# Grouping small matrix products by the shape of the array's parts in a three-block network

## The chip, the cores and the metric

The kernel runs on one core of one Trainium2 chip. The metric is the device time of one execution in microseconds (us). TensorE (PE) multiplies matrices: a weight load (PEld) puts the left operand into the array, a matmul streams the right operand through it. VectorE (DVE), ScalarE (ACT) and GpSimd (POOL) work beside it, and SyncE (SP) issues the transfers. Every engine takes its instructions in the order of the program.

## The reference

The network has three parts over 512 tokens of 1024 features, all in float32: a block with neighbourhood attention, a short convolution and an MLP; a layer of RWKV-7 time mixing between two gated MLPs; and a layer of sliding-window attention with sinks between two gated MLPs. The change concerns the RWKV scan above all. Its recurrence, per head of 64 features (16 heads):

```
def step(S, inp):
    r_t, w_t, k_t, v_t, kk_t, b_t = inp
    sa = jnp.einsum('bhij,bhj->bhi', S, -kk_t)
    S = (S * w_t[:, :, None, :] + sa[..., None] * b_t[:, :, None, :]
         + v_t[..., None] * k_t[:, :, None, :])
    y = jnp.einsum('bhij,bhj->bhi', S, r_t)
    return S, y
```

Around it stand the projections of r, k, v, low-rank decays and gates, a group norm per head, and an output projection.

## The kernel before

Activations lie with features on the 128 partitions and tokens along the free axis. The large products split each float32 operand into a high and a low part of a faster type (`wh`, `wl` for weights; three products for one); in the trace these are the rows `m<-a,wh`, `m<-a,wl`, `m<-wh,a`. Here they are called the main products.

The scan is done in chunks of 64 tokens (`c` = 0 to 7) for each half of the heads (`q` = 0, 1), so in 16 steps. A half of the heads is four pairs `p`, and a pair is two heads `e` = 0 and 1, which lie on partitions 0 to 63 and 64 to 127. There are three parts, each a task of its own:

- Block preparation, `prep(q, j)` for each block `j` of 128 tokens (lines 1354 to 1430). VectorE makes the scaled operands `bk` and `ee` (the tile `E[q, e, cg]`) for a chunk; TensorE multiplies them, four products per head (line 1404, operands on 64 partitions, 128 columns); VectorE masks the result into `ARB` and `E`. There are 16 such chunks, with eight products each.
- `inverse(j)` (lines 1445 to 1505): GpSimd inverts small triangular blocks in 62 operations, transfers bring the result through DRAM (`fsc`, `iat`, `xsc`), and TensorE joins the blocks with products of 32 x 32. The scan of block `j` waits for it.
- `scan_task(q)` (lines 1568 to 1649). A step makes a right-hand side (line 1595, eight products), multiplies with the inverse (line 1603, eight), makes the next state (line 1620, eight), and the output `y` of the chunk (lines 1636 to 1641): for each head and pair one product with 128 rows and 64 columns of the array (`ee` with `sv`) and, added to it, one with 64 rows and 64 columns (`ARB` with `uv`). So `y` has eight products of each of the two shapes. The two heads' outputs lie in two banks of PSUM, on the same 64 partitions. Such a float32 product has two records in the trace.

In the RWKV part all this runs among the main products of the projections, and later among those of the following MLP. The order on TensorE is set before the run by a planner, the class `_Emit`: it follows a coarse clock for TensorE and lanes for the others, and resumes a task when its clock reaches the time at which the tiles that the task named are expected. `mm` (line 363) and `transpose` (line 375) advance TensorE's clock by a duration that they state; so a changed duration can move every instruction of the program. A framework below it, which schedules by priority, may still move single instructions.

Of the kernel before, what the change touches and what calls it, by code (L numbers as in the profile page):

```python
# [13 lines left out]
F32R = mybir.dt.float32r  # L14
# [4 lines left out]
PSUM = bass.MemoryType.PSUM  # L19

P = 128
T = 512
D = 1024
# [37 lines left out]
class _Lane:  # L61
    """the busy spans of an engine; an operation takes the time that is free from when it is ready"""
# [25 lines left out]
class _Emit:  # L88
    """Order of emission for TensorE, which runs its instructions in the order in which they are emitted.

    A coarse model follows when each tile's contents will be there. The main thread of matrix products
    advances the clock of TensorE; side tasks are generators that yield a delay, or the tiles that their
    next instructions need, and are resumed when the clock gets there."""
# [4 lines left out]
    def __init__(self):  # L98
# [6 lines left out]
        self.urgent = 0  # L105

# [14 lines left out]
    def avail(self, aps):  # L121
        """when TensorE can read, or for a bank of PSUM write, these"""
        return max((self.slot.get(ap.tensor.name, 0.0) if ap.space == PSUM else self.ready([ap]) for ap in aps), default=0.0)

    def new(self, ap, tag):
        """a tile's slot is free once the tile that had it is done with"""
# [24 lines left out]
    def gate(self, outs, t):  # L151
        """tiles of a tag get their slots in the order of emission"""
        return max([t] + [self.seq.get(ap.tensor.tag, 0.0) for ap in outs if self.is_new(ap)])
# [49 lines left out]

    def pe(self, out, ins, dur):
# [33 lines left out]
    def need(self, *aps):  # L238
        """side tasks take the time until these tiles are ready"""
# [16 lines left out]
class _Engine:  # L256
    """an engine whose instructions the emission's model follows"""
# [25 lines left out]
def tile_net(ctx: ExitStack, tc: tile.TileContext, a: dict, out: bass.AP, dbg=None, stop=None):  # L283
# [26 lines left out]
    def free(*tiles, n=0):  # L310
        """these tiles of apool have had their last use, and n unnamed ones"""
# [15 lines left out]
    def PS(side=None):  # L327
        """a bank of PSUM; those of the side tasks are apart, for banks are handed out in the order of emission"""
# [33 lines left out]

    def mm(out_, lhsT, rhs, start=True, stop=True):
# [5 lines left out]
        em.pe(out_, [lhsT, rhs], 0.0025 + (max(n, 2 * m if m > 64 else m) if rhs.dtype == F32R else max(n, m) * (3 if m == 64 else 4)) / 2400.0)  # L369
# [6 lines left out]
    def transpose(out_, in_):  # L376
        nc.tensor.transpose(out_, in_, ident[: in_.shape[0], : in_.shape[0]])  # L377
        em.pe(out_, [in_], 0.11)

# [37 lines left out]
    def gemm(ps, w, n, ks, xs, cols=FULL, first=None, last=None, eng=None):  # L417
        """ps[:, cols] += W[ks, row block n]^T @ xs[cols] for a weight laid out [n, 128, k * 128]"""
# [7 lines left out]
    def gemm_head(w, ns, xs, ready):  # L426
        """the first row blocks of a product, a half of the tokens at a time as xs becomes ready"""
# [12 lines left out]
    def gemm_n(pss, w, xs, js=range(4), ncol=512, first={}):  # L440
        """token-major: pss[j] = xs[:, block j]^T @ W for W laid out [128, k * ncol]; first: those of W loaded before"""
# [14 lines left out]
    def rsqrt_(y, v, tmp):  # L456
        """y = v ** -0.5 (v > 0) on small tiles"""
# [7 lines left out]
    class Stat:  # L465
        """sum of squares over features, and from it each token's (mean + eps) ** -0.5"""
# [52 lines left out]
    def when(cond, fn):  # L519
        """run fn once cond holds"""  # L520
# [6 lines left out]
    def attention(units, depth):  # L527
        """softmax attention, a few units of a head and a block of queries in flight; a unit is a generator"""
# [13 lines left out]
    # =====================================================================  # L542
    # first block (tokens column-major: t' = col * 8 + row)
    # =====================================================================
# [1582 lines left out]
```

## Time and profile before

| | us |
|---|---|
| median of 3 runs | 3050.56 (3047.28 to 3051.03) |
| span of the profiled execution, first to last instruction | 3042.9 |
| TensorE busy | 2896.4 (95%) |
| VectorE busy | 1630.0 (54%) |
| ScalarE busy | 1255.6 (41%) |
| GpSimd busy | 694.0 (23%) |

The profiled execution has its own time as a span alone; it lies 7.7 us below the median of the runs. Matmuls overlap in the array, so the start of the next row tells more of a product's cost than its own duration. From about 1060 to 1800 us the RWKV layer runs; before and after it lie attention and MLPs.

### The profile page before, as it was taken

Reading aid. Unit: us, or ns where it says so; the run is one execution under the profiler, and the core shown is the slowest. Engines: PE = TensorE matmul, PEld = TensorE weight load, DVE = VectorE, ACT = ScalarE, POOL = GpSimd, SP = SyncE. Lnnn points to the kernel's source line nnn. Section 1 sums busy time; section 2 is a strip of 40 time slices with the busy share of each in tenths; the row PEclk is TensorE's granted clock in tenths of the full one; section 3 lists DMA queues with packets and bytes.
Section 4 is the critical chain, followed back from the end, with each engine's and each line's share of the span. In section 5 each row is a group of like instructions: output and inputs, shape, how many; then the busy total and the mean of one; then the engine's idle time right before and its main releaser. Section 6 shows DMA issues by size and latency. Waiting matters only on the chain. (4 is left out here: it accounts for less than half of the span.)

```text
span 3042.9 us, 45860 instructions
## 1 busy us (share of the span) xinstructions
PE 2896.4 (95%) x17744; PEld 2490.5 (82%) x17744; DVE 1630.0 (54%) x2920; ACT 1255.6 (41%) x2205; POOL 694.0 (23%) x809
## 2 busy tenths in 40 slices
PE   9999999999999988888889999998999989899998
PEld 7788988889788876667678999998888886788887
DVE  6554443335334596855774575457334475752336
ACT  4532333333433345544454444344323347643333
POOL 0011211112211153562173110011111135320111
PEclk9999999999999989897888999999999999999999
DMA  5333333332233456554564455442333433323334
GB/s 177 86 97 97 111 97 97 97 97 91 90 98 125 127 180 198 180 154 141 161 190 118 158 171 178 124 158 84 111 99 123 122 101 84 97 82 100 107 111 156
DMA packets 179409, 378.32 MB, mean 124 GB/s; under 512 B 57204, under 2 KB 81908, under 8 KB 179192
## 3 DMA queue, kind: packets, MB, share of 16 engines
q1 hardware_dynamic: 179192, 375.40, 40.0%
q8 instruction: 140, 2.29, 0.3%
q14 instruction: 77, 0.63, 0.1%
HBM read 342.04 MB, written 29.36 MB: 122 GB/s over the span
## 5 line engine op out<-in xcount | busy, mean ns | idle before, releaser
L364 PE MATMUL m<-a,wh 128*128 128x256 f32 (+1 forms) x8512 | 2075.8, 335 | 13.6 <-DVE a L275 5.9
L364 PEld LDWEIGHTS m<-a,wh 128*128 128x128 f32 x8512 | 1469.0, 193 | 179.3 <-issue 10.9
L364 PE MATMUL m<-a,wl 128*128 128x256 f32 (+1 forms) x4256 | 1418.6, 334 | 1.0 <-DVE wl L275 1.0
L275 ACT ACTIVATE wh<-wr 128x1024 fp32r<-128x1024 f32 (+2 forms) x585 | 606.4, 1038 | 1228.6 <-PE m L364 855.6
L275 DVE TENSOR_TENSOR wl<-wr,wh 128x1024 fp32r<-128x1024 f32 (+2 forms) x547 | 674.9, 1236 | 480.2 <-ACT wh L275 477.2
L364 PEld LDWEIGHTS m<-a,wl 128*128 128x128 f32 x4256 | 819.6, 193 | 78.1 <-issue 2.4
L275 POOL TENSOR_TENSOR a<-a,a 128x256 f32<-128x256 f32 (+5 forms) x319 | 363.6, 1147 | 1552.6 <-ACT a L275 1328.6
L275 DVE TENSOR_TENSOR a<-m,a 128x512 f32<-128x512 f32 (+1 forms) x324 | 208.7, 645 | 642.2 <-PE m L364 624.5
L275 ACT ACTIVATE a<-a 128x512 f32<-128x512 f32 (+6 forms) x531 | 253.1, 494 | 127.5 <-DVE a L275 108.2
L364 PE MATMUL m<-wh,a 128*128 128x512 f32 x800 | 269.3, 410 | 16.7 <-ACT a L275 8.7
L364 PEld LDWEIGHTS m<-wh,a 128*128 128x128 f32 x800 | 155.7, 195 | 56.6 <-ACT a L275 10.2
L275 DVE TENSOR_TENSOR a<-a,a 128x256 f32<-128x256 f32 (+3 forms) x305 | 174.6, 598 | 28.9 <-ACT a L275 22.2
L364 PE MATMUL m<-wl,a 128*128 128x512 f32 x400 | 161.6, 404 | 3.7 <-DVE wl L275 2.3
L275 DVE SCALAR_TENSOR_TENSOR a<-a,vec,a 128x256 f32<-128x256 f32 (+4 forms) x246 | 144.7, 628 | 8.6 <-ACT a L275 8.3
L275 POOL TENSOR_TENSOR a<-h,a 128x256 fp32r<-128x256 f32 x80 | 68.6, 861 | 302.6 <-ACT a L275 294.4
L275 POOL TENSOR_TENSOR wl<-wr,wh 128x1024 fp32r<-128x1024 f32 x38 | 93.8, 2471 | 143.5 <-ACT wh L275 136.7
L364 PE MATMUL t<-a,a 64*128 64x128 f32 (+3 forms) x400 | 85.1, 358 | 14.6 <-DVE a L275 12.9
L364 PEld LDWEIGHTS m<-wl,a 128*128 128x128 f32 x400 | 78.5, 196 | 20.8 <-DVE wl L275 3.4
L364 PE MATMUL t<-sv,a 128*64 128x64 f32 x992 | 89.5, 245 | 0.0
L364 PEld LDWEIGHTS t<-sv,a 128*64 128x64 f32 x992 | 67.4, 142 | 23.4 <-issue 3.8
L275 ACT ACTIVATE a<-t 128x512 f32<-128x512 f32 (+3 forms) x122 | 58.9, 491 | 65.5 <-PE t L364 53.5
L364 PEld LDWEIGHTS t<-a,a 64*128 64x128 f32 (+2 forms) x400 | 54.4, 204 | 33.3 <-issue 19.8
(109 smaller groups left out, 1595.5 us busy)
## 6 DMA issues: line engine op xcount, KB each, us to landing
wr<-in_ffn_w_in_dram SPq DMA_DIRECT2D x204, 512.0 KB, 3.6
wr<-in_ffn_w_out_dram SPq DMA_DIRECT2D x80, 448.0 KB, 3.3
wr<-in_ffn_w_out_dram SPq DMA_DIRECT2D x48, 512.0 KB, 3.5
wr<-in_w_out_t_dram SPq DMA_DIRECT2D x34, 512.0 KB, 3.3
wr<-in_w_mlp_in_dram SPq DMA_DIRECT2D x32, 512.0 KB, 3.6
wr<-in_w_mlp_out_dram SPq DMA_DIRECT2D x32, 512.0 KB, 3.7
wr<-in_w_gate_dram SPq DMA_DIRECT2D x16, 512.0 KB, 3.5
wr<-in_w_k_dram SPq DMA_DIRECT2D x16, 512.0 KB, 5.1
```

The costliest lines, as they stand in the source:

```text
L275: return fn(*args, **kw)
L364: nc.tensor.matmul(out_, lhsT=lhsT, rhs=rhs, start=start, stop=stop)
```

## The change

In the scan, the 16 products of a step's output are written in another order: first the eight with 128 rows, then the eight with 64 rows, the two heads alternating in each. The accumulation's start stands at the first pair alone and its stop at the last. In the block preparation, the eight products of a chunk are issued after one wait for both heads' operands, the heads alternating, into two banks. And the planner's price of a product changes: a new function adds 0.09 us where the shape of the array's part differs from that of the product before, and halves the duration where the shape is the same and the place another; the discount for 64 columns goes. Comments were removed as well, which shifts the line numbers (the products' line 364 is 377 now, the transposes' 377 is 391).

```diff
+        self.shape, self.pos = (128, 128), (0, 0)
...
+    def tile_time(self, out, lhsT, dur):
+
+        rows, cols = (ap.ap[0][1] for ap in (lhsT, out))
+        shape = (64 if rows == 64 else 32 if rows <= 32 else 128, 64 if cols == 64 else 32 if cols <= 32 else 128)
+        pos = (lhsT.offset // lhsT.ap[0][0], out.offset // out.ap[0][0])
+        if shape != self.shape:
+            dur += 0.09
+        elif pos != self.pos:
+            dur *= 0.5
+        self.shape, self.pos = shape, pos
+        return dur
...
-        em.pe(out_, [lhsT, rhs], 0.0025 + (max(n, 2 * m if m > 64 else m) if rhs.dtype == F32R else max(n, m) * (3 if m == 64 else 4)) / 2400.0)
+        dur = 0.0025 + (max(n, 2 * m if m > 64 else m) if rhs.dtype == F32R else n * 4) / 2400.0
+        em.pe(out_, [lhsT, rhs], em.tile_time(out_, lhsT, dur))
...
-        em.pe(out_, [in_], 0.11)
+        em.pe(out_, [in_], em.tile_time(out_, in_, 0.11))
...
+                yield (bk, *(E[q, e, cg] for e in range(2)))
+                pas = [PS(), PS()]
+                for p in range(4):
+                    for e in range(2):
+                        pr = slice(64 * e, 64 * e + 64)
+                        mm(pas[e][:, p * 128 : (p + 1) * 128], bk[pr, p * 128 : (p + 1) * 128], E[q, e, cg][pr, p * 128 : (p + 1) * 128])
                 for e in range(2):
                     pr, qr = slice(64 * e, 64 * e + 64), slice(64 - 64 * e, 128 - 64 * e)
                     ee = E[q, e, cg]
-                    pa = PS()
-                    yield (pa, bk, ee)
-                    for p in range(4):
-                        mm(pa[:, p * 128 : (p + 1) * 128], bk[pr, p * 128 : (p + 1) * 128], ee[pr, p * 128 : (p + 1) * 128])
-                    p4 = pa.rearrange("p (q f) -> p q f", q=4)
+                    p4 = pas[e].rearrange("p (q f) -> p q f", q=4)
...
-                for e in range(2):
-                    hr = slice(64 * e, 64 * e + 64)
-                    for p in range(4):
-                        yo = py[e][par * 64 : par * 64 + 64, p * 64 : p * 64 + 64]
-                        mm(yo, ee[e][:, p * 128 + 64 : p * 128 + 128], sv4[:, p, e, :], True, False)
-                        mm(yo, ARB[q, j][hr, (par * 4 + p) * 64 : (par * 4 + p + 1) * 64], uv4[hr, p, e, :], False, True)
+
+                def yo(e, p):
+                    return py[e][par * 64 : par * 64 + 64, p * 64 : p * 64 + 64]
+
+                for p in range(4):
+                    for e in range(2):
+                        mm(yo(e, p), ee[e][:, p * 128 + 64 : p * 128 + 128], sv4[:, p, e, :], p == 0, False)
+                for p in range(4):
+                    for e in range(2):
+                        hr = slice(64 * e, 64 * e + 64)
+                        mm(yo(e, p), ARB[q, j][hr, (par * 4 + p) * 64 : (par * 4 + p + 1) * 64], uv4[hr, p, e, :], False, p == 3)
```

How the change moves the instructions shows in the program's order. The first place is TensorE at the last output of the scan; `sv2762` and `sv2764` are the step's two right operands (`sv` and `uv`), `t2729` and `t2730` the banks of the two heads. Before:

```order
L364 MATMUL t2729_14756<-sv2762_14969,a2484_13270 64x64
L364 MATMUL t2729_14756<-sv2764_14990,a2455_13123 64x64
L364 MATMUL t2729_14756<-sv2762_14969,a2484_13270 64x64
L364 MATMUL t2729_14756<-sv2764_14990,a2455_13123 64x64
L364 MATMUL t2729_14756<-sv2762_14969,a2484_13270 64x64
```

The same output in the changed kernel, around the border of its two halves (`sv2744` and `sv2746` are `sv` and `uv`, `t2719` and `t2720` the two heads' banks):

```order
L377 MATMUL t2719_14681<-sv2744_14854,a2476_13197 64x64
L377 MATMUL t2720_14682<-sv2744_14854,a2479_13209 64x64
L377 MATMUL t2719_14681<-sv2744_14854,a2476_13197 64x64
L377 MATMUL t2720_14682<-sv2744_14854,a2479_13209 64x64
L377 MATMUL t2719_14681<-sv2746_14875,a2432_13034 64x64
L377 MATMUL t2720_14682<-sv2746_14875,a2432_13034 64x64
```

Before, the shape changes at every product; now it changes once, and the heads alternate. Of the 16 outputs 12 stand so in the changed program; of the four in the middle (steps 4 to 7) parts are split into runs of four by head.

The second place is TensorE at two chunks of the block preparation in the changed kernel. In an early one (`t1749` and `t1750` are the two heads' banks) the heads alternate:

```order
L377 MATMUL t1749_9870<-a1721_9771,a1720_9770 128x128
L377 MATMUL t1750_9871<-a1724_9782,a1720_9770 128x128
L377 MATMUL t1749_9870<-a1721_9771,a1720_9770 128x128
L377 MATMUL t1750_9871<-a1724_9782,a1720_9770 128x128
L377 MATMUL t1749_9870<-a1721_9771,a1720_9770 128x128
```

In a late one (`t2493` and `t2494` are the two heads' banks) they don't:

```order
L377 MATMUL t2493_13277<-a2476_13197,a2475_13196 128x128 x4
L377 MATMUL m2517_13399<-a2215_12002,wh2519_13401 128x256
L377 MATMUL m2517_13399<-a2214_12001,wl2520_13402 128x256
L377 MATMUL m2517_13399<-a2214_12001,wh2519_13401 128x256
L377 MATMUL t2494_13278<-a2479_13209,a2475_13196 128x128 x4
```

Of the 16 chunks the heads alternate throughout in five, all of the first half of the tokens, and partly in three; in eight they stay in two runs of four, as all 16 do before.

The third place is TensorE at the inverse of the third block (`inverse(2)`), whose first products are the 32 x 32 ones. Before, they stand far inside the MLP's main products:

```order
L364 MATMUL m2598_13891<-a2523_13459,wh2600_13893 128x256 x2
L364 MATMUL m2598_13891<-a2523_13459,wl2601_13894 128x256
L364 MATMUL m2598_13891<-a2525_13468,wh2600_13893 128x256 x2
L364 MATMUL t2545_13553<-cst_75,a2543_13549 32x32 x16
L364 MATMUL m2598_13891<-a2525_13468,wl2601_13894 128x256
```

In the changed kernel they stand ahead of the MLP's main products, among the products of a norm's statistics (`t2525`, `t2533`):

```order
L377 MATMUL m2517_13399<-a2215_12002,wh2519_13401 128x256
L377 MATMUL m2517_13399<-a2214_12001,wl2520_13402 128x256
L377 MATMUL t2521_13418<-a2497_13304,cst_75 128x512
L377 MATMUL t2525_13444<-cst_75,a2384_12847 128x1 x2
L377 MATMUL t2508_13347<-cst_75,a2506_13343 32x32 x16
L377 MATMUL t2533_13493<-h2526_13459,cst_75 128x256
L377 MATMUL t2530_13486<-h2529_13483,a2192_11885 32x32 x16
```

Between the last products of the block preparation that this inverse needs and its first 32 x 32 products stood 344 main products before; now 192 stand there, and the others come later.

## Rows read from the trace of the kernel before

**Rows 1.** The page's head, engines, and slices (PE busy and clock granted, in tenths).
```profile
span 3042.9 us, 45860 instructions
PE 2896.4 (95%) x17744; PEld 2490.5 (82%) x17744; DVE 1630.0 (54%) x2920; ACT 1255.6 (41%) x2205; POOL 694.0 (23%) x809
...
PE   9999999999999988888889999998999989899998
...
PEclk9999999999999989897888999999999999999999
```
**Rows 2.** Busy time by stretch: start:end, length, engines (us), clock, DMA share, GB/s.
```profile
1060.00:1336.00 276.00, 223.94 (x1265) 180.30 (x1264) 223.10 (x399) 132.75 (x258) 140.62 (x177) 0.88 0.59 184
1336.00:1410.00 74.00, 73.62 (x913) 60.44 (x914) 28.64 (x65) 35.95 (x82) 27.71 (x47) 0.95 0.42 125
1410.00:1482.00 72.00, 63.26 (x434) 46.19 (x433) 50.53 (x84) 28.90 (x56) 19.43 (x15) 0.81 0.54 166
1482.00:1595.00 113.00, 87.99 (x638) 76.80 (x638) 92.65 (x202) 63.82 (x139) 57.23 (x104) 0.86 0.59 182
1595.00:1710.00 115.00, 114.28 (x1332) 99.28 (x1329) 53.46 (x110) 47.22 (x97) 34.83 (x59) 0.91 0.42 121
```
**Rows 3.** Groups by shape of the products that change: shape, records, busy us, mean ns.
```profile
L364 PE MATMUL t<-sv,a 128*64 128x64 f32 x736 | 62.7, 242 | 0.0
...
L364 PE MATMUL t<-sv,a 64*64 64x64 f32 x256 | 43.6, 253 | 0.0
L364 PE MATMUL t<-a,a 64*128 64x128 f32 x256 | 40.4, 312 | 14.0 <-DVE a L275 12.9 <-ACT h L275 1.0
```
**Rows 4.** Timeline of PE, the last output: start us, duration us, operation, records.
```profile
1704.68 0.28 PE L364 MATMUL m<-a,wl 128*128 128x256 f32 x1
1704.89 4.32 PE L364 MATMUL t<-sv,a 128*64 128x64 f32 x32
1709.14 0.79 PE L364 MATMUL m<-a,wh 128*128 128x256 f32 x2
```
**Rows 5.** Timeline of PE: eight products whose places alternate.
```profile
1595.97 0.69 PE L364 MATMUL t<-sv,a 128*64 128x64 f32 x16
1596.59 0.38 PE L364 MATMUL m<-a,wh 128*128 128x256 f32 x1
```
**Rows 6.** Timeline of PE: block preparation, four products of one head at one place.
```profile
1297.92 1.16 PE L364 MATMUL t<-a,a 64*128 64x128 f32 x8 [1.40 <-DVE a L275]
1299.01 1.01 PE L377 MATMUL t<-cst,a 128*128 128x128 f32 x4
```
**Rows 7.** Waits of PE, 1482 to 1595 us: who waited for whom, us, times, longest.
```profile
PE t L364 <- DVE a L275: 15.0, 3, 7.9
PE m L364 <- ACT a L275: 5.6, 2, 5.3
```
**Rows 8.** Timeline of PE and of DVE where the first half's scan has ended.
```profile
1481.90 1.23 DVE L275 TENSOR_TENSOR wl<-wr,wh 128x1024 fp32r<-128x1024 f32 x1 [3.96 <-ACT wh L275]
...
1488.20 2.04 PE L364 MATMUL t<-a,a 64*128 64x128 f32 x8 [6.06 <-DVE a L275]
```
**Rows 9.** Timelines around the third inverse: PE, POOL (first, last), SP, PE, main products.
```profile
1508.62 1.16 PE L364 MATMUL t<-a,a 64*128 64x128 f32 x8
...
1528.62 0.65 POOL L275 TENSOR_TENSOR h<-a,iat 128x31 f32<-128x31 f32 x1 [16.28 <-DMA gd<-h]
...
1565.00 1.42 POOL L275 TENSOR_TENSOR a<-a,h 128x16 f32<-128x16 f32 x1
...
1584.26 1.00 SPq L275 DMA_DIRECT2D a<-xsc  x2
...
1589.81 0.40 PE L364 MATMUL m<-a,wh 128*128 128x256 f32 x2
...
1590.17 0.40 PE L364 MATMUL m<-a,wh 128*128 128x256 f32 x2
...
1590.86 0.69 PE L364 MATMUL t<-cst,a 32*32 32x32 f32 x32
...
1555.86 1.01 PE L364 MATMUL t<-cst,a 128*128 128x1 f32 x4 [7.87 <-DVE a L275]
```
**Rows 10.** Timeline of PE at the first inverse.
```profile
1322.30 1.06 PE L364 MATMUL t<-cst,a 32*32 32x32 f32 x32 [8.17 <-DMA a<-xsc]
```

## The prediction

> **What bounds the kernel now.** I read the page's head first: TensorE is busy for 2896.4 of 3042.9 us, and seven slices in a row are below 9 tenths, the fifteenth to the twenty-first (1065 to 1598 us), where the RWKV layer runs [rows 1]. Outside that layer nothing but TensorE can be the bound. Then I cut the layer into stretches [rows 2]. The reader is to see two kinds. In 1336 to 1410 us (the first half's steps 1 to 4) TensorE is busy for 73.62 of 74.00 us, and in 1595 to 1710 us (all eight steps of the second half) for 114.28 of 115.00: there what TensorE no longer does comes off the end, as long as main products stand between the steps to cover their waits. In 1060 to 1336 us it idles for 52 of 276 us and in 1482 to 1595 us for 25 of 113, while VectorE is busy for 223 and 93: there the block preparation sets the pace, and a shorter product waits. 1410 to 1482 us (steps 5 to 8) lies between, with 9 us idle, and the wait right after it is one for VectorE.
>
> Third come the groups by shape [rows 3]: 256 records of 64 x 64 are the second half of the output, the same number of the 736 of 128 x 64 the first half, 256 of 64 x 128 the block preparation. Two records are a product, so there are 128 of each. Their mean durations, 242 to 312 ns, don't tell the cost, since such products overlap; the starts of successive rows do.
>
> **The output's products.** An output of 16 products takes from 1704.89 to 1709.14, 4.25 us or 0.27 us a product [rows 4]; in it the shape changes at each. Eight products of 128 x 64 whose two heads go to different columns take from 1595.97 to 1596.59, 0.62 us or 0.08 each [rows 5]. Four products of one head at one place, 64 x 128, take from 1297.92 to 1299.01, 1.09 us or again 0.27 each [rows 6], though no shape changes within them; but they are twice as wide in the loaded columns and in the streamed ones.
>
> The new output has eight products of 128 rows whose outputs lie on the same 64 partitions for both heads: one place, so no alternation in the array. No row shows this. Its bounds are 0.62 us (they overlap like those of [rows 5]) and 8 x 0.27 = 2.2 us (they cost what those of [rows 6] do). I take the row of [rows 6], nearest in being at one place, at half its width: 0.14 us a product, and for eight 1.1 us. The eight of 64 rows alternate between the upper and the lower rows of the array, into two banks. No row has that with shared columns; the bounds are the same, and I take 0.62 us, for in [rows 5] alternation alone gives it. The new output costs 1.1 + 0.62 = 1.7 us, saving 2.5 us; the bounds of the saving are 3.0 (both 0.62) and -0.2 (both 2.2).
>
> The order tells how often the program has it so: in 12 of the 16 steps. In the others the output stands in four runs of four products of one head. Each begins with a change of shape, which I put at 0.1 us, an estimate from 0.27 us a product in [rows 4] against the 0.14: 16 x 0.14 + 4 x 0.1 = 2.6 us, saving 1.7.
> - Second half, eight clean steps, on TensorE's full stretch: 8 x 2.5 = 20.0 us (bounds 24 and -1.6).
> - Steps 1 to 4, three clean and one in runs, in the other full stretch: 3 x 2.5 + 1.7 = 9.2 us (bounds 12 and -1).
> - Steps 5 to 8, three in runs and one clean: 3 x 1.7 + 2.5 = 7.6 us. At their end TensorE waits 6.06 us for VectorE, and VectorE has just waited 3.96 us for ScalarE, whose buffers TensorE frees [rows 8]. So a part comes through and a part turns into a longer wait. I take half, 3.8 us (bounds 0 and 7.6).
>
> These steps are paid on the critical engine only while something is left to run: after the change 471 main products stand between the second half's first inverse products and its last output, 409 before. So the chain from step to step (a copy, a product, a sum) has more cover, not less.
>
> Here a page of the Trainium skill speaks against the change: "TensorE: Matmul & The Clock Gate", Part 3, under "The mechanism", says that a weight load runs beside a matmul in flight only where the two use different groups of rows. The first eight products use all rows. By it the saving would be that of the first rival below. The trace disagrees as far as it goes: the products of [rows 5] use all rows too and cost 0.08 us. At one place no run here shows it.
>
> **The block preparation.** Two runs of four cost 2 x 1.09 = 2.2 us a chunk [rows 6]; eight that alternate would cost about 1.1. By the order, five chunks of 16 alternate throughout and three in part: 5 x 1.1 + 3 x 0.5 = 7 us less work. All of it lies where TensorE idles for 52 and 25 us [rows 2], and what hides it is VectorE's work on the next chunk. I count nothing (bounds 0 and 7, the latter if VectorE is ahead). The one wait for both heads delays the first head's four products by VectorE's work on the second head. Behind them on TensorE stand main products, which wait with them; in the stretches where VectorE sets the pace anyway I count that at nothing (bounds -3 and 0).
>
> **The planner's moves.** With new prices the whole RWKV part is ordered anew. The largest move is the third inverse. Its GpSimd work ends at 1566.4 us, 58 us after the last products that it needs (1508.62); its last transfer is issued at 1584.26, late, behind others in SP's queue; TensorE comes to it at 1590.86, 82 us after those products, and doesn't wait [rows 9]. Three main products take 0.36 us there, 0.12 each. So 344 main products were 41 us of the 82, waits about 10 [rows 7], other products 31. Now 192 main products stand there: 23 + 31 = 54 us of work, 64 with the old waits. The result can be there after 58 us and two transfers of up to 6.6 us each (1584.26 to 1590.86 for issue, landing and arrival), 71 us; at worst after the old 82. So TensorE may stand for about 7 us (bounds 0 and 18 to 28). Against that, the wait of 7.87 us for the norm's statistics in the same place [rows 9] may be partly covered, since inverse and scan come next instead of the MLP that hangs on it; at the first inverse 131 main products stand for 107 before, so its wait of 8.17 us [rows 10] shrinks by up to 5. Taken together -2 us (bounds -28 and +15). Outside the RWKV layer some attention units move by a few products, on a full TensorE: 0, within 3 us.
>
> **The sum.** 20.0 + 9.2 + 3.8 + 0 - 2 = 31 us. The profiled execution's span would be 3042.9 - 31 = 3012 us. The median of the runs lies 7.7 above that span, so the runs would give 3050.6 - 31 = 3020 us.
>
> **Rivals.**
> - Products at one place overlap less. If each costs 0.27 us whatever its width, the eight of 128 rows take 2.2 us and a clean output 2.8, saving 1.4; runs of four save nothing. That is 8 x 1.4 + 3 x 1.4 + half of 1.4 - 2 = 14 us: 3036 us. For it: [rows 4] and [rows 6] show the same 0.27 us at one place, with and without a change of shape. Against it: the widths differ by two.
> - The new order fills waits. VectorE's work gets ahead with the faster TensorE, and of the 52, 9 and 25 us of idle time some 15 go, with steps 5 to 8 and the preparation counted in full (3.8 + 7): 31 + 26 = 57 us at most, about 50 and so 3000 us in the middle. For it: the two long waits of [rows 9] and [rows 10]. Against it: VectorE's amount of work is the same.
> - The saving turns into waits: the steps become bound by their own chain or by VectorE, and of 31 us some 5 are left: 3045 us. For it: VectorE is busy for four fifths of the stretches around. Against it: in the two full stretches VectorE is busy for only 39% and 46% [rows 2].
> - Slower: TensorE stands at the inverses of the second half. The planner puts them 18 us earlier than their result if that comes 82 us after the products as before; the fourth inverse follows on the same GpSimd queue. From the point where both stand for 18 us or more, 36 us go against 33 saved, and the main products behind them lose the loads that queue on SP behind the inverse's transfers, some 5 us more: 3058 us. Against it: 24 of the 82 us were SP's queue and TensorE's own lateness, not GpSimd's work.
>
> That the change doesn't do what it says is partly so already, as the order shows (four outputs and eleven chunks), and is in the sum.
>
> **How the numbers follow.** 0.47 for the forecast (its own range 3011 to 3030), 0.17 for less overlap, 0.16 for filled waits, 0.13 for a saving turned into waits, 0.07 for slower. 0.2% is 6 us, about what can be told from no change. Faster by more: 0.47 + 0.17 + 0.16 and a third of 0.13, 0.84; within: 0.09; slower: 0.07. The range from 3000 to 3042 reaches the middle of the filled waits and, on the other side, all of the first rival and the edge of the next.
>
> **What would show it.** In the changed profile an output should take 1.7 us from its first row to the next; 2.8 would be the first rival, 1.2 the upper bound. TensorE should be full in both scan stretches, the second one about 20 us shorter for the same work. The preparation's alternating chunks should take about 1.1 us, with the waits for VectorE around them not shorter in sum. A wait on the inverse's transfers of over 10 us in the second half would show the slower rival at work; waits of TensorE in the layer, 87 us in the five stretches of [rows 2], that grow by the saving would show the third.

## The result and the profile after

The changed kernel takes 3022.81 us (median of 4 runs, 3018.23 to 3025.78) against 3048.92 us of the kernel before on the same chip (4 runs, 3043.59 to 3051.03): a ratio of 0.9914, with a 95% interval from 0.9896 to 0.9931. The profiled execution has a span of 3016.5 us, 26.4 us under that of before [rows 1].

The page's head, its engines and two of its slices (PE busy, clock granted, in tenths), of the changed kernel:

```profile
span 3016.5 us, 45856 instructions
...
PE 2855.6 (95%) x17744; PEld 2458.6 (82%) x17744; DVE 1628.5 (54%) x2920; ACT 1255.9 (42%) x2205; POOL 690.3 (23%) x809
...
PE   9999999999999988788889999998999989899998
...
PEclk9999999999999999899779999999999999999999
```

TensorE is busy for 40.8 us less, but the span is only 26.4 us shorter: 14 us of what it saved became waits. The groups by shape show where it was saved (columns as in [rows 3]):

```profile
L377 PE MATMUL t<-a,a 64*128 64x128 f32 x256 | 39.2, 346 | 27.3 <-DVE a L288 15.8 <-ACT a L288 11.4
L377 PE MATMUL t<-sv,a 128*64 128x64 f32 x736 | 38.3, 229 | 1.1 <-issue 0.8 <-ACT h L288 0.4
...
L377 PE MATMUL t<-sv,a 64*64 64x64 f32 x256 | 12.9, 224 | 0.0
```

The two groups that hold the output fell from 62.7 and 43.6 us to 38.3 and 12.9, together by 55 us (such records overlap, so TensorE as a whole saves less); that of the block preparation from 40.4 to 39.2, and the waits ahead of it grew from 14.0 to 27.3 us. An output's own time, in the timeline of TensorE (start, duration, operation, records), is the distance from its row to the next:

```profile
1670.98 0.28 PE L377 MATMUL m<-a,wl 128*128 128x256 f32 x1
1671.19 1.75 PE L377 MATMUL t<-sv,a 128*64 128x64 f32 x32
1672.88 0.50 PE L377 MATMUL m<-a,wh 128*128 128x256 f32 x2
```

That is 1.69 us, where [rows 4] had 4.25. Two stretches of the layer answer to the last two of [rows 2]: between the halves of the scan, and the second half's scan (columns as there):

```profile
1482.00:1580.00 98.00, 78.96 (x577) 66.52 (x577) 68.37 (x146) 50.48 (x118) 47.47 (x100) 0.71 0.54 153
1580.00:1674.00 94.00, 92.38 (x1269) 86.71 (x1270) 58.82 (x123) 48.80 (x94) 38.38 (x60) 0.97 0.59 165
```

The second half's scan still fills TensorE (92.38 of 94.00 us). Two neighbouring steps with 54 main products in each show what a step gives: in the kernel before, their outputs (in rows of 64 records) begin 12.66 us apart (TensorE's timeline):

```profile
1665.56 5.26 PE L364 MATMUL t<-sv,a 128*64 128x64 f32 x64
...
1678.22 5.26 PE L364 MATMUL t<-sv,a 128*64 128x64 f32 x64
```

In the changed kernel

```profile
1596.81 2.84 PE L377 MATMUL t<-sv,a 128*64 128x64 f32 x64
...
1607.05 2.85 PE L377 MATMUL t<-sv,a 128*64 128x64 f32 x64
```

they begin 10.24 us apart, 2.4 less, the same 134 records at full clock in both. Between the halves TensorE idles for 19 us, not 25, but at a mean granted clock of 0.71 instead of 0.86. The six largest groups of TensorE's waits over the whole layer (who waited for whom: us, times, longest):

```profile
PE t L377 <- DVE a L288: 24.8, 17, 5.4
PE t L377 <- ACT a L288: 11.7, 6, 5.7
PE t L377 <- POOL a L288: 11.1, 4, 6.8
PE m L377 <- DVE a L288: 10.4, 6, 3.9
PE m L377 <- POOL a L288: 9.4, 5, 6.4
PE t L377 <- DMA a<-xsc: 7.6, 1, 7.6
```

One wait on an inverse's transfer is there, that of the first inverse (7.6 us, 8.17 in [rows 10]); none in the second half. The third inverse moved from 1590.86 to 1556.8 us and what it waits behind is VectorE:

```profile
1555.88 2.00 PE L377 MATMUL t<-cst,a 128*128 128x1 f32 x36 [5.13 <-DVE a L288]
```

(Its row merges two products of the norm's statistics with the inverse's 32 records.)

For a common measure of all kernels I count the main products along the timeline (those into `m`, 14022 in each) and take the RWKV layer from the 4801st to the 7301st. TensorE has 5216 to 5223 records in it in every kernel, so the work is the same; only the stretch differs. Busy time by stretch (columns as in [rows 2]), first of the kernel before:

```profile
1050.60:1790.31 739.71, 647.15 (x5222) 546.06 (x5221) 516.24 (x997) 358.07 (x719) 296.98 (x417) 0.89 0.54 164
```

and of the changed kernel:

```profile
1054.90:1762.86 707.96, 601.90 (x5223) 512.21 (x5222) 511.70 (x997) 358.21 (x719) 294.33 (x417) 0.90 0.58 172
```

The layer is 31.8 us shorter: TensorE is busy for 45.3 us less and idle for 13.5 us more (106.1 for 92.6). Of these, 13.3 us lie ahead of the preparation's products (27.3 for 14.0, the groups above and [rows 3]). Ahead of the layer 4.3 us are lost (it begins at 1054.90 for 1050.60), and 1.1 us behind it.

### The profile page after: what moved, and what is told of

It reads as the page before. It is cut to its first block, busy times and chain, and to the rows that moved or that the text cites. A ratio compares the mean times of both kernels' runs of the same rounds, so it can differ in the third digit from the quotient of the medians.

```text
span 3016.5 us, 45856 instructions
## 1 busy us (share of the span) xinstructions
PE 2855.6 (95%) x17744; PEld 2458.6 (82%) x17744; DVE 1628.5 (54%) x2920; ACT 1255.9 (42%) x2205; POOL 690.3 (23%) x809
## 5 line engine op out<-in xcount | busy, mean ns | idle before, releaser
L288 DVE TENSOR_TENSOR a<-a,a 128x256 f32<-128x256 f32 (+3 forms) x305 | 159.6, 550 | 24.0 <-ACT a L288 17.2
L288 POOL TENSOR_TENSOR wl<-wr,wh 128x1024 fp32r<-128x1024 f32 x38 | 92.6, 2438 | 134.4 <-ACT wh L288 116.7
L288 ACT ACTIVATE a<-a,vec 128x256 fp32r<-128x256 f32 (+2 forms) x108 | 60.3, 565 | 41.4 <-DVE a L288 39.2
L377 PE MATMUL t<-cst,a 32*32 32x32 f32 (+2 forms) x432 | 34.7, 237 | 41.4 <-POOL a L288 25.3
```

The costliest lines, as they stand in the source:

```text
L288: return fn(*args, **kw)
L377: nc.tensor.matmul(out_, lhsT=lhsT, rhs=rhs, start=start, stop=stop)
```

## The experiments

My theory: the gain is TensorE's time on the output, by grouping the shapes, and comes through where TensorE is full; prices and preparation are worth about nothing. The first rival: the new order that the prices make brings the gain. The second: the alternating heads in the preparation share in it. Each time is given as a ratio to the kernel before in the same session, with its 95% interval.

**The parts apart.** The planner resumes a waiting task some time, its slack, after the task's tiles are expected. With the old prices it has no order for the new output at a scan task's slack of 2.0 us, but has one at 2.1, so a control with 2.1 stands beside it.

```diff
-SLACKS = {"gn_task": 6.0, "prep": 2.5, "scan_task": 2.0}
+SLACKS = {"gn_task": 6.0, "prep": 2.5, "scan_task": 2.1}
```

> The kernel before with one number changed: a scan task is given a slack of 2.1 instead of 2.0, with the old prices, so the order around the scan moves a little. It is the control for the run with the output alone, which can't be ordered at 2.0. Every theory expects the time of the kernel before within 6 us, 3043 to 3055 us; an output of the second half still takes 4.25 us from its first row to the next.

Measured: 3041.23 us, ratio 0.9976 (0.9958 to 0.9993), 7 us under the kernel before (2 to 13) where every theory had at most 6: a small miss. Its twelve runs go from 3029.97 us, at a granted clock of 0.967 (mean of the whole execution), to 3048.01 us at 0.959, and the profiled execution (span 3029.9 us, 0.968) lies near the lower end. An output takes 4.10 us from its row to the next, at full clock (the 4.25 of [rows 4] held a piece at half clock):

```profile
1692.52 4.18 PE L364 MATMUL t<-sv,a 128*64 128x64 f32 x32
1696.62 0.50 PE L364 MATMUL m<-a,wh 128*128 128x256 f32 x2
```

The output alone is the control with the output's part of the change's diff.

> The new order of the 16 output products alone (old prices, old block preparation, slack 2.1 as in the control); outside the output 15477 of the 15688 products of TensorE that remain stand in the order of the control. My theory (the gain is TensorE's time on the output, and comes through where TensorE is full): an output takes 1.7 us instead of 4.25, and the kernel is 20 to 28 us faster than the control, most of it in the second half's scan. Rival A (the planner's new order makes the gain): the outputs are shorter but the time is within 8 us of the control. Rival B (the alternating heads in the preparation share in it): under 18 us.

Measured: 2999.38 us, ratio 0.9838 (0.9813 to 0.9863). Against the control that is 1.38% or 42 us, with some 9 us of uncertainty either way (the two intervals combined): more than the 20 to 28 that I had expected, and far from what either rival allows. The layer's row:

```profile
1050.86:1746.41 695.55, 606.11 (x5221) 521.42 (x5220) 510.87 (x994) 356.57 (x717) 298.96 (x417) 0.89 0.58 173
```

Beside the control's (725.93 us, 638.36 busy, 0.90) it is 30.4 us shorter, of which 32.3 are busy time; idle time is up by 1.9. Counted along the main products, the output alone is 12.4 us ahead of the control at the 6001st (some 30 us behind the last output of the first half) and 30.8 at the 7301st. So the saving comes through whole: 31 us between the two profiled executions, 42 between the medians. The difference goes with the granted clock: the output alone has 0.966 to 0.970 in its four runs, and the control's five runs at 0.965 or more have a median of 3031.65 us, 32 us above it. And the part alone beats the whole change by 23 us (0.76%, with 0.31 of uncertainty).

The prices alone: the new `tile_time` and its calls, output and preparation as before.

> The planner's new prices alone; output and preparation are written as before. My theory: no gain, the time of before within 6 us, or up to 6 us slower, because the loss of some 4 us that the changed kernel has up to 860 us (the attention and MLP ahead of the RWKV layer) comes from the order that these prices make. Rival A (the new order, with the third inverse and the second half's scan earlier, makes the gain): 12 to 26 us faster than before.

Measured: 3060.97 us, ratio 1.0048 (1.0030 to 1.0066), 15 us slower than before. My theory had at most 6, and the rival a gain; both miss. The layer's row:

```profile
1054.56:1806.36 751.80, 664.53 (x5222) 560.60 (x5221) 511.85 (x997) 358.58 (x719) 295.16 (x417) 0.86 0.54 162
```

It is 12.1 us longer than before for the same records. Idle time is not up (87.3 for 92.6); busy time is, by 17.4 us, at a granted clock of 0.86 for 0.89. At 1.2 GHz instead of 2.4 that is about 2 x 0.14 x 752 = 210 us for about 163. All nine runs show it: the clock of the whole execution is 0.955 to 0.960, in the twenty runs of the kernel before beside them 0.959 to 0.969. The other 4 us are lost ahead of the layer, 2.6 of them between the 300th and the 380th main product (from 88 us on): these take 54.9 us in every kernel with the old prices there and 57.5 to 57.8 in every one with the new. The rest is no more than kernels with the old prices there differ by among themselves: their layers begin at 1049.00 to 1052.03 us.

Prices and output, with the preparation as before:

```diff
-                yield (bk, *(E[q, e, cg] for e in range(2)))
-                pas = [PS(), PS()]
-                for p in range(4):
-                    for e in range(2):
-                        pr = slice(64 * e, 64 * e + 64)
-                        mm(pas[e][:, p * 128 : (p + 1) * 128], bk[pr, p * 128 : (p + 1) * 128], E[q, e, cg][pr, p * 128 : (p + 1) * 128])
                 for e in range(2):
...
+                    pa = PS()
+                    yield (pa, bk, ee)
+                    for p in range(4):
+                        mm(pa[:, p * 128 : (p + 1) * 128], bk[pr, p * 128 : (p + 1) * 128], ee[pr, p * 128 : (p + 1) * 128])
```

> New prices and the new output, the block preparation written as before (four products of a head after a wait of its own). My theory (the preparation is worth nothing): the time of the changed kernel within 6 us, 3017 to 3029 us. Rival B (the alternation in the preparation matters): 7 us or more slower than the changed kernel, since eight chunks of it alternate; or, if the one wait for both heads costs more than the alternation gives, up to 6 us faster.

Measured: 3029.8 us, ratio 0.9931 (0.9908 to 0.9953). The preparation's part is the difference to the changed kernel, 0.17% or 5 us with 9 us of uncertainty: not told from nothing, nor from the 7 us of rival B. Its group shows two parts:

```profile
L377 PE MATMUL t<-a,a 64*128 64x128 f32 x256 | 42.2, 322 | 18.7 <-DVE a L288 16.9 <-ACT a L288 1.9
```

With the changed preparation it is 39.2 us, 3 us less work, but the waits ahead of it are 27.3 us, 8.6 more. Output and prices multiply out: 0.9862 (output alone over control) x 1.0048 = 0.991, within the uncertainty of the 0.993 measured for both together.

**What in the output saves the time.** Three variants of the output alone, with old prices (the third at a slack of 2.0). The first lets the shape change after every two products, the heads still alternating.

```diff
                 for p in range(4):
                     for e in range(2):
-                        mm(yo(e, p), ee[e][:, p * 128 + 64 : p * 128 + 128], sv4[:, p, e, :], p == 0, False)
-                for p in range(4):
+                        mm(yo(e, p), ee[e][:, p * 128 + 64 : p * 128 + 128], sv4[:, p, e, :], True, False)
                     for e in range(2):
...
-                        mm(yo(e, p), ARB[q, j][hr, (par * 4 + p) * 64 : (par * 4 + p + 1) * 64], uv4[hr, p, e, :], False, p == 3)
+                        mm(yo(e, p), ARB[q, j][hr, (par * 4 + p) * 64 : (par * 4 + p + 1) * 64], uv4[hr, p, e, :], False, True)
```

> The run with the output alone (old prices, slack 2.1), with one thing undone: the shape changes after every two products (both heads' 128 x 64, both heads' 64 x 64, and so on), while the heads still alternate. 15679 of the 15688 other products keep their places. Theory S (a change of shape costs some 0.15 us, which is what grouping removes): an output holds 7 changes instead of 1 and takes about 1.7 + 6 x 0.15 = 2.6 us, 0.9 us more; sixteen of them 14 us, the kernel 8 to 15 us slower than the output alone. Rival H (what helps is that the two heads alternate, not the shapes): 1.7 to 2.0 us an output and the kernel within 5 us of the output alone.

Measured: 3013.07 us, ratio 0.9887 (0.9869 to 0.9906), above the output alone by 15 us (with 9 of uncertainty) in the ratios and by 13.4 in the spans. An output takes 2.55 us:

```profile
1681.63 2.62 PE L377 MATMUL t<-sv,a 128*64 128x64 f32 x32
1684.18 0.50 PE L377 MATMUL m<-a,wh 128*128 128x256 f32 x2
```

Six more changes of shape cost 2.55 - 1.69 = 0.86 us, 0.14 us each. Sixteen outputs make 13.8 us, about what the span grew by: theory S, at its number. The edit also moves the accumulation's start and stop, but those don't make the price: at a change of shape some 150 ns pass to the next record's start in the control, in the output alone and here, whichever flags the products have.

The second keeps the shapes grouped and sets the heads one behind the other, in both pairs of loops.

```diff
-                for p in range(4):
-                    for e in range(2):
+                for e in range(2):
+                    for p in range(4):
```

> The run with the output alone (old prices, slack 2.1), with the shapes grouped but the heads not alternating: eight of 128 x 64 and eight of 64 x 64, four of one head and then four of the other in each. The order moves around it (13609 of 15688 other products keep their places), so it is judged first by the output's own time. Theory S: the first eight stay at 1.1 us (one place in both), the second eight go from 0.5 to about 1.0 us, since four in a row lie at one place; an output takes 2.2 us, 0.5 more, sixteen of them 8 us. Rival H (alternation is what matters): 4 us an output, as before. If places don't matter at all: 1.7 us.

Measured: 3005.26 us, ratio 0.9856 (0.9835 to 0.9876). An output takes 1.97 us, 0.28 more than alternating:

```profile
1669.47 2.04 PE L377 MATMUL t<-sv,a 128*64 128x64 f32 x32
1671.44 0.50 PE L377 MATMUL m<-a,wh 128*128 128x256 f32 x2
```

Theory S has the sign, and the size is half of the 0.5 expected; the kernel's 5 us over the output alone, with 10 of uncertainty, aren't told from nothing. Of the 2.4 us that the new output saves at full clock, the alternation makes 0.28 and the grouping the other 2.1.

The third puts the second head's output on the other 64 partitions, so that the 128 x 64 products alternate too; the norm's task copies that head in two pieces.

```diff
-            for e in range(2):
-                copy(y4[:, :, e, :], py[e].rearrange("p (q d) -> p q d", q=4))
+            copy(y4[:, :, 0, :], py[0].rearrange("p (q d) -> p q d", q=4))
+            for i in range(2):
+                copy(y4[64 * i : 64 * i + 64, :, 1, :], py[1].rearrange("p (q d) -> p q d", q=4)[64 - 64 * i : 128 - 64 * i])
...
-                    return py[e][par * 64 : par * 64 + 64, p * 64 : p * 64 + 64]
+                    r0 = 64 * (par ^ e)
+                    return py[e][r0 : r0 + 64, p * 64 : p * 64 + 64]
```

> The output alone with old prices (slack 2.0), and the second head's output on the other 64 partitions, so that the eight products of 128 x 64 alternate between the columns of the array as well; the norm's task then copies the second head in two halves. The other products: 15036 of 15688 as in the output alone. Theory S (products at alternating places start at twice the pace): the first eight go from 1.1 to about 0.6 us, an output takes 1.2 us instead of 1.7, sixteen of them 8 us; less some for the third copy, the kernel is 3 to 8 us faster than the output alone. Rival (the pace of such products is set by something else than the place, or another order takes the gain back): an output at 1.7 us, or the kernel within 3 us of the output alone or slower.

Measured: 3002.06 us, ratio 0.9851 (0.9832 to 0.9870). An output takes 1.23 us:

```profile
1663.26 1.30 PE L377 MATMUL t<-sv,a 128*64 128x64 f32 x32
1664.49 0.50 PE L377 MATMUL m<-a,wh 128*128 128x256 f32 x2
```

The output's time is as theory S says, the kernel's as its rival says: no faster than the output alone (4 us slower, with 10 of uncertainty). Sixteen outputs should give 7 us; in its layer TensorE is busy for 1.8 us less (604.3 for 606.1) and idles for 5.5 more (94.9 for 89.4). Its order was another one and its norm has a copy more, so what took the rest isn't settled.

**Why the prices cost time.** Theory P: they make a worse order as such. Rival L: this order is one throw, which any small number shifts. The changed kernel with a slack of 2.1 instead of 2.0 for a scan task (the edit of the control):

> The changed kernel with the slack of a scan task at 2.1 instead of 2.0: the same prices, another order (14416 of 15688 products outside the output keep their places). The prices alone cost 16 us, and the changed kernel lies 23 us above the output alone. Theory P (the prices as such make the worse order): within 8 us of the changed kernel, 3015 to 3031 us, well above the output alone. Rival L (the prices were one throw of an order that any small number shifts by 10 us and more): more than 8 us away from the changed kernel, on either side.

Measured: 3025.89 us, ratio 0.9928 (0.9911 to 0.9945): 3 us from the changed kernel, with another order. That is as theory P has it, though one other order is a thin test.

The new prices in the RWKV layer alone:

```diff
-        dur = 0.0025 + (max(n, 2 * m if m > 64 else m) if rhs.dtype == F32R else n * 4) / 2400.0
-        em.pe(out_, [lhsT, rhs], em.tile_time(out_, lhsT, dur))
+        if em.tiled:
+            dur = 0.0025 + (max(n, 2 * m if m > 64 else m) if rhs.dtype == F32R else n * 4) / 2400.0
+            dur = em.tile_time(out_, lhsT, dur)
+        else:
+            dur = 0.0025 + (max(n, 2 * m if m > 64 else m) if rhs.dtype == F32R else max(n, m) * (3 if m == 64 else 4)) / 2400.0
+        em.pe(out_, [lhsT, rhs], dur)
...
+        em.tiled = True
```

> The changed kernel, with the new prices used in the RWKV layer alone; outside it the old ones. Its first 5220 products stand exactly as with the old prices. Theory: the 3 to 4 us that all runs with the new prices have lost up to 860 us come from the order there, so they return and nothing else changes: 3015 to 3021 us. Rival (that loss is made good later anyway, or the layer's order moves with it): 3021 to 3030 us.

Measured: 3024.4 us, ratio 0.9920 (0.9903 to 0.9937). The loss ahead of the layer returns (the 4801st main product begins at 1050.94 us, not 1054.90), but the layer is 14.0 us longer in this profile than in the changed kernel's, at a clock of 0.88 for 0.90. The rival's time, then; whether the layer's part is its slightly other order or a less lucky execution, one profile doesn't tell (the changed kernel's was the fastest of its four runs).

Then theory W: the prices that the trace contradicts do the harm. One price is mended, that of one-column products:

```diff
-        dur = 0.0025 + (max(n, 2 * m if m > 64 else m) if rhs.dtype == F32R else n * 4) / 2400.0
+        dur = 0.0025 + (max(n, 2 * m if m > 64 else m) if rhs.dtype == F32R else max(n, m) * 4) / 2400.0
```

> The changed kernel with one price as before: a product that streams one column (128 x 1, 56 of them, for norms and statistics) is priced at 0.22 us again instead of 0.004; the trace measures 0.27 from start to start. Theory W (the prices that the trace contradicts make the worse order): 5 to 20 us faster than the changed kernel. Rival P (new prices cost what they cost, whichever single one is mended): within 5 us of it, or slower.

Measured: 3026.73 us, ratio 0.9936 (0.9919 to 0.9954). (The median from the start of such a product to the next start, without waits, is 0.22 us in the trace; 0.27 is the mean duration of one of its two records.) Then the halving:

```diff
         elif pos != self.pos:
-            dur *= 0.5
+            dur *= 1.0
```

> The changed kernel without the halving of a price where the place alternates (the 0.09 us for a change of shape stays). In the trace the 64 x 128 products of the block preparation take 0.29 us against a price of 0.13 with the halving and 0.22 without; the 32 x 32 ones 0.05 against 0.034 and 0.056. Theory W: 5 to 20 us faster than the changed kernel. Rival P: within 5 us of it, or slower.

Measured: 3030.26 us, ratio 0.9943 (0.9926 to 0.9961). And both edits together:

> The changed kernel with both prices mended: one-column products at 0.22 us and no halving, so that of the kinds of products none is priced at under half of what the trace measures. Theory W: the time of the output alone with old prices, or near it, 2997 to 3010 us. Rival P (a price nearer to the measured time doesn't by itself make a better order): 3015 us or more.

Measured: 3036.0 us, ratio 0.9966 (0.9956 to 0.9977), 0.52% or 16 us above the changed kernel; the two intervals don't meet. Theory W falls: each price nearer to the trace left the kernel as slow or made it slower. The layer with both mended idles most of all kernels, and its longest wait is one of main products for ScalarE:

```profile
1053.85:1789.86 736.01, 612.18 (x5222) 526.63 (x5221) 516.66 (x997) 355.66 (x719) 295.59 (x417) 0.86 0.55 165
```

```profile
PE m L377 <- ACT a L288: 24.6, 5, 14.0
PE t L391 <- POOL a L290: 13.8, 5, 7.4
```

The layer of all fourteen kernels, read from the same view (one profiled execution each; idle is length less busy). The last column is the granted clock of the whole execution, median and range of all runs of that kernel:

| Kernel | prices | layer, us | TensorE busy | idle | clock | clock of all runs |
|---|---|---|---|---|---|---|
| before | old | 739.7 | 647.2 | 92.6 | 0.89 | 0.964 (0.959 to 0.969) |
| control, slack 2.1 | old | 725.9 | 638.4 | 87.6 | 0.90 | 0.963 (0.959 to 0.969) |
| output alone | old | 695.6 | 606.1 | 89.4 | 0.89 | 0.967 (0.966 to 0.970) |
| shapes alternate | old | 708.2 | 618.4 | 89.8 | 0.90 | 0.967 (0.964 to 0.967) |
| heads apart | old | 703.0 | 612.4 | 90.6 | 0.89 | 0.967 (0.967 to 0.971) |
| columns | old | 699.2 | 604.3 | 94.9 | 0.89 | 0.968 (0.967 to 0.968) |
| prices alone | new | 751.8 | 664.5 | 87.3 | 0.86 | 0.958 (0.955 to 0.960) |
| prices and output | new | 724.4 | 627.7 | 96.8 | 0.86 | 0.962 (0.961 to 0.965) |
| changed kernel | new | 708.0 | 601.9 | 106.1 | 0.90 | 0.964 (0.963 to 0.967) |
| changed, slack 2.1 | new | 720.8 | 616.7 | 104.2 | 0.87 | 0.964 (0.962 to 0.966) |
| new prices inside only | new | 721.9 | 612.8 | 109.1 | 0.88 | 0.962 (0.961 to 0.964) |
| one-column price mended | mended | 723.2 | 609.5 | 113.8 | 0.88 | 0.964 (0.963 to 0.966) |
| halving off | mended | 726.2 | 617.9 | 108.3 | 0.87 | 0.961 (0.961 to 0.962) |
| both mended | mended | 736.0 | 612.2 | 123.8 | 0.86 | 0.962 (0.960 to 0.963) |

That the prices cost time doesn't hang on one order: the seven kernels with the new output and new or mended prices take 3022.81 to 3036.0 us, the three with grouped shapes and old prices 2999.38 to 3005.26.

How they cost it is in part the clock. With the new output its median over all runs is 0.967 or 0.968 in the four kernels with old prices and 0.961 to 0.964 in the seven with new or mended ones. An estimate for the changed kernel, from its 0.964: 2 x 0.003 x 3020 = 18 us more at 1.2 GHz instead of 2.4, or 9 us where TensorE is the bound, of the 23 between it and the output alone.

The idle time isn't put down to the prices so easily. The two kernels with new prices and the old preparation idle for 87.3 and 96.8 us, those with old prices for 87.6 to 94.9. Over 100 us stand only in the six kernels with the changed preparation, whose products wait once for both heads; in the changed kernel the growth lies ahead of those products. No run has the changed preparation with the old prices, so its share and that of the prices aren't separated, and in the kernel with both prices mended other waits have grown too. Which of the planner's decisions costs the clock stays open.

## Why the prediction was right, and where it was not

The time came within 3 us of the forecast, and the fall was 26 us where 31 were put; but two of its terms were off, and in opposite directions.

- **The output's cost** (4.25 to 1.7 us) held: 1.69. The choice of the row at one place, 0.14 us a product, was close: successive records of the eight 128 x 64 products start 58 ns apart, 0.12 us a product. The first rival (products at one place overlap less, 3036 us) had 2.8 us an output and is out. The page "TensorE: Matmul & The Clock Gate" of the Trainium skill, Part 3, "The mechanism", lets a weight load run beside a matmul only on other groups of rows. In the run with columns the 128 x 64 products use all rows, and each pair of records starts 6 to 7 ns apart and the pairs 58 ns, as with alternating rows: the trace disagrees.
- **The estimate of a change of shape**, 0.1 us, was low: 0.14. The Trainium skill's page "TensorEngine Tiling (Array Packing)", under "Key Properties", says that a change of the tiling mode drains TensorE, and one of place doesn't; the trace agrees in that only the first costs time, 0.14 us.
- **The three terms of the output**, 20.0 + 9.2 + 3.8 = 33 us, were to come through in full in the second half, and by half in steps 5 to 8. The output alone gives 30.8 us in the profiles (12.4 for 13.0 up to a point between the halves of the scan, 18.4 for 20.0 behind it) and 42 with 9 of uncertainty in the runs. The reason was right, and so was the place; the size lies at the foot of what the runs allow.
- **The preparation at nothing** stands as a total, which isn't told from nothing, but not in its parts: 3 us less work where 7 were put, and 8.6 us more waiting in front of its products (one profile each), where the one wait for both heads had a bound of 3. A chunk whose heads alternate (TensorE's timeline of the changed kernel, around its wait for VectorE):

```profile
1216.49 0.46 PE L377 MATMUL t<-a,a 64*128 64x128 f32 x2 [0.32 <-DVE a L288]
1217.95 1.13 PE L377 MATMUL t<-a,a 64*128 64x128 f32 x14 [1.01 <-DVE a L288]
1219.01 0.66 PE L391 MATMUL t<-cst,a 128*128 128x128 f32 x4
```

  Seven products took 1.06 us (eight were put at 1.1), and a wait of 1.01 us stands inside the chunk.
- **The planner's moves at -2 us** is the step that failed. The prices alone cost 15 us (9 to 20). That lies inside the bounds, 28 lost to 15 gained, but it came about in another way than the one that set them. I had worked out one place, the third inverse, and there TensorE doesn't stand at the transfers, so the rival that was slower is out too. What the prices alone cost in the layer is clock: 17.4 us more busy time for the same records, at 0.86 for 0.89, with no more idle time (87.3 for 92.6 us). I had no term for a layer ordered anew as a whole. What I had priced at 0, within 3 us, the attention ahead, lost 2.6, within its bound.
- The second rival, filled waits, is out: idle time is 106.1 for 92.6 us in the changed kernel. The output alone, at 2999 us, is where it had put the time, but not by its mechanism: idle time is 89.4 us there, in its control 87.6. "VectorE's amount of work is the same" was an argument against filled waits; it should have been weighed as one for more of them, too. The third, the saving turned into waits, is partly what happened: 13.5 of 45.3 us, though ahead of the preparation's products and not in the scan's steps.

So the sum of 31 us came out near by luck: a loss of about 15 that I had at 2 was met by an output whose worth in the runs lay some 9 above the 33 that I had, with an interval that reaches down to 33. The granted clock, for which the sum has no term, is in both: its median over the runs is 0.967 for the output alone and 0.963 for its control, 0.958 for the prices alone, and 0.964, as before, for the whole change.

## What to carry to other kernels

Small products on parts of the array are worth grouping by shape first, and alternating in place second: here 2.1 us an output against 0.28, and 0.46 more where the 128 x 64 products alternate too. Take a change that touches both the work and the numbers that order it apart, and time the parts: here the new order of the output's products alone gave 31 to 42 us, and the whole change 23 us less than that part; new prices for the planner alone cost 15. A planner's price that is nearer to the trace is not thereby better; its numbers are set for an order, and have to be judged by the idle time and the clock of the stretch that they order, over several runs, since the clock differs from one run to the next.

## What the runs showed of the hardware

- A change of the part's shape costs 0.14 us between products of 64 columns (six more of them in an output, 0.86 us), and from the control to heads apart, with 14 fewer, (4.10 - 1.97) / 14 = 0.15 us. In the records of the outputs of the control and the output alone: at one shape successive records start 58 ns apart, or in pairs 58 ns apart where the places alternate; the first record of another shape starts some 150 ns after the last one, and the next at its place 107 ns behind it.
- Alternating the columns doubles the pace of products that use all 128 rows (1.69 to 1.23 us an output), the same as alternating the rows.
- One program's runs differ with the granted clock: the control's twelve go from 3029.97 us at 0.967 to 3048.01 at 0.959. So the clock of one profile isn't yet that of an order. In the layer of the changed kernel TensorE is busy for 601.9 us at 0.90, with prices and output, the same output, for 627.7 at 0.86; but over all their runs the two kernels' clocks (0.963 to 0.967, 0.961 to 0.965) and times (3018.23 to 3025.78 us, 3018.13 to 3030.93) overlap. For the prices alone the lower clock stands in all nine runs.
